# Sixty-seven elementwise operations move from GpSimd to the VectorE in two attention mixers, and the exponential's table is loaded at their start

## The chip, the cores and the metric

One core of a Trainium2 chip runs the whole program. The metric is device time in microseconds (us) of one execution; three executions of the kernel before took 1954.1 to 1957.93 us. [...]

## The reference, cut to what matters

Two transformer layers on 512 tokens of width 1024, all in f32: each layer is half an FFN, a mixer, and half an FFN. The first mixer is "even" (sparse NSA attention beside dilated attention), the second is MLA.

```python
for l in range(2):
    x = x + 0.5 * _swiglu(_rms_norm(x, ffn1_norm[l]), ...)
    h = _rms_norm(x, mix_norm[l])
    x = x + (_even_mixer(h, ...) if l % 2 == 0 else _mla_mixer(h, ...))
    x = x + 0.5 * _swiglu(_rms_norm(x, ffn2_norm[l]), ...)
return _rms_norm(x, final_norm)

def _rope(x, cos, sin):            # rotary positions
    x1, x2 = x[..., :half], x[..., half:]
    return concatenate([x1 * c - x2 * s, x2 * c + x1 * s])

def _probs(scores, mask):          # softmax; every attention uses it
    s = where(mask, scores, -MASK_BIG)
    p = where(mask, exp(s - max(s)), 0)
    return p / sum(p)
```

In the even mixer, 8 NSA heads attend to compressed keys (31 blocks), to selected blocks and to a window; 8 more heads are a mixture of three dilated branches. MLA has 16 heads with low-rank queries and keys.

## The kernel before, in words

Everything is kept transposed: `x` is eight tiles of 128 features x 512 tokens. A matmul in f32 accuracy is three matmuls (`mm3`, lines 150 to 154) on a high part and a low part of both operands. So every operand is split first: ScalarE copies it to the rounded type (`wh`, `qh`, `oh`, ...), and then another engine subtracts that copy from the tile (`wl`, `ql`, `ol`, ...). For weights this is `fetch` (lines 136 and 137).

The stages run in order: FFN, even mixer, FFN, FFN, MLA mixer, FFN, norm. An FFN keeps TensorE on long rows of 128x512 matmuls. A mixer is a software pipeline, `pipe` (line 313): for each head it emits the next head's scores and softmax (`soft`), then the units of work that a plan written by hand (`EVEN`, `MLA`, lines 34 to 46) puts beside this head (projections of queries and keys, values, the compression, output projections), then this head's transposes (`trans`) and its product with the values (`pv`). What is emitted last goes through a scheduler that may move instructions on each engine by its own timing model; each engine then runs its list strictly in order.

Softmax of a head and a block of 128 queries: TensorE writes scores into one of two `pb` banks; the VectorE adds the mask and takes the minimum (line 273, an operation and a read of its accumulator, tile `mn`), which frees the bank; ScalarE takes the exponential (276); the VectorE takes a reciprocal (277); GpSimd scales (281). Other PSUM banks: `pa` (2, projections, queries, output projection), `pt` (3, transposes), `pc` (1, the heads' outputs).

What GpSimd does besides 281, by line:

- `rope` (427): the VectorE multiplies the projection by the cosines (430) and shuffles it (431); GpSimd multiplies the shuffled tile by the sines (432) and adds both (433). 15 calls.
- `finish` (473): a pair of heads is split for the output projection, low part on GpSimd (483). 8 pairs.
- `cmp_probs` (570), twice: softmax on compressed keys. VectorE 583 to 586, exponential on ScalarE (587), product with the mask on GpSimd (588), sum, reciprocal and gate on the VectorE (589 to 592), product with the gate on GpSimd (595), transposes on TensorE (598).
- MLA: one product in the keys' rotary part (650), the low part of a query (708, 16 times) and of a pair of heads (726, 8 times).
- `stack` adds positions for the compression (520, eight operations), `squares` sums squares for the norms (174); both stay.

`out_proj` (381) writes pieces of the output into the two `pa` banks; the VectorE adds each to `x` (397), and the bank is free again. ScalarE loads a table for the exponential before the first exponential of each mixer, at line 276, and one for silu in the FFN after it (238).

Of the kernel before, what the change touches and what calls it, by code (L numbers as in the profile page):

```python
# [3 lines left out]
P = 128  # L4
D, SEQ, FF = 1024, 512, 2816
KT, NF, HF = D // P, FF // P, FF // P // 2
# [17 lines left out]
def raw(ap):  # L24
    return ap.bitcast(F32)
# [46 lines left out]
class Core:  # L72
# [137 lines left out]

    def norm(self, gi):
        xs = [self.split(self.x[k], self.g[:, gi * 8 + k:gi * 8 + k + 1], "x", 8) for k in range(KT)]
        col, row = self.rms(self.x)
        return xs, col, row
# [185 lines left out]
    def even(self, gi):  # L400
        nc, a, kp = self.nc, self.a, self.keep
        with self.tc.tile_pool(name="ev", bufs=1, reuse_waits="tile") as sb:
            xs, rc, R = self.norm(gi)
            CR = sb.tile([P, SEQ], F32, name="CR")
# [22 lines left out]
            def rope(p):  # L427
                t = self.tmp()
                s = self.tmp()
                nc.vector.tensor_tensor(t, p, CR, OP.mult)  # L430
                nc.vector.stream_shuffle(s, p, SHUF8)
                nc.gpsimd.tensor_tensor(s, s, SR, OP.mult)
                nc.gpsimd.tensor_tensor(t, t, s, OP.add)
                return t
# [38 lines left out]
            def finish(pair, j):  # L473

                def f(ps):
                    if j == 0:
                        O[pair] = kp.tile([P, SEQ], F32, name="of")
                    self.fold(sb, ps, O[pair][64 * j:64 * j + 64])
                    if j == 1:
                        h = sb.tile([P, SEQ], F32R, name="oh", bufs=4)  # L480
                        l = sb.tile([P, SEQ], F32R, name="ol", bufs=4)
                        nc.scalar.activation(h, O[pair], AF.Copy)
                        nc.gpsimd.tensor_tensor(l, O[pair], raw(h), OP.subtract)
                        oh[pair] = h, l
                return f
# [84 lines left out]
            def cmp_probs(g):  # L570
# [8 lines left out]
                st = C["st"][g]  # L579
# [8 lines left out]
                nc.gpsimd.tensor_tensor(t, t, mcmp[:, 1].unsqueeze(2).to_broadcast([P, 4, 4, 32]), OP.mult)  # L588
# [6 lines left out]
                nc.gpsimd.tensor_tensor(t, t, sp(st[:, 2]), OP.mult)  # L595
# [22 lines left out]
    def mla(self, gi):  # L618
        nc, a, kp = self.nc, self.a, self.keep
        with self.tc.tile_pool(name="ml", bufs=1, reuse_waits="tile") as sb:  # L620
            xs, rc, R = self.norm(gi)

# [19 lines left out]
            def low(i):  # L642
# [3 lines left out]
                if i == 3:  # L646
# [3 lines left out]
                    nc.gpsimd.tensor_tensor(s, s, cs[:, 1], OP.mult)  # L650
# [46 lines left out]
            def query(h):  # L697
# [10 lines left out]
                nc.gpsimd.tensor_tensor(ql, t, raw(qh), OP.subtract)  # L708
                qs[h] = qh, ql

            def attend(h):
# [5 lines left out]
                def after(ps):  # L717
# [4 lines left out]
                    if j == 1:  # L722
# [3 lines left out]
                        nc.gpsimd.tensor_tensor(l, O[pair], raw(x), OP.subtract)  # L726
# [153 lines left out]
```

## Time and profile before

| | |
|---|---|
| median of three runs | 1957.92 us |
| the runs | 1957.92, 1954.1, 1957.93 us |
| the profiled execution | 1958.47 us |
| its span, first to last instruction | 1956.7 us |
| its mean granted TensorE clock | 0.993 |
| busy in the span: TensorE, VectorE, ScalarE, GpSimd | 1916.9, 1057.6, 754.9, 407.7 us |

The stages lie about here in the span: FFN to 376 us, even mixer to 684, two FFNs to 1398, MLA mixer to 1592, FFN to 1940, final norm to 1957. A row of a window names the stretch and its length, then for each engine the time in which it was busy with its number of instructions, the granted clock, and the share and rate of the DMA engines. A row of a timeline has the start, the time from start to end, the engine, the line and what it writes from what; in brackets the idle time before it. A row of a wait has the total, the number of waits and the longest. Operations on the VectorE that follow each other without a wait start a little before the one ahead has ended, so that rows overlap by some hundredths of a us. Ends of matmuls are modelled.

### The profile page before, as it was taken

How to read it: one execution, taken by the hardware profiler on the slowest of the kernel's cores; microseconds unless marked ns; L12 is line 12 of the kernel's file. 1: busy time of each engine (PE TensorE's matmuls, PEld its weight loads, DVE VectorE, ACT ScalarE, POOL GpSimd, SP SyncE). 2: the span in 40 equal slices, each digit the busy share in tenths (PEclk: the TensorE clock that was granted, in tenths of full speed). 3: DMA queues.
4: the chain of work that ended last, by engine and by line, in shares of the span. 5: the costliest groups of instructions: out<-in, count | busy, mean ns of one | idle time of the engine just before them, and what ended most of it. 6: DMA issues, size and time to landing. Idle time of an engine off the chain costs nothing.

```text
span 1956.7 us, 23295 instructions
## 1 busy us (share of the span) xinstructions
PE 1916.9 (98%) x9086; PEld 1604.4 (82%) x9086; DVE 1057.6 (54%) x1594; ACT 754.9 (39%) x1230; POOL 407.7 (21%) x390
## 2 busy tenths in 40 slices
PE   8999999999999999999999999999999999999997
PEld 6888888878897888888888888888878878888886
DVE  5543444467788754434544543554399765434442
ACT  5321323347586532222333322333388643212231
POOL 4110111164355311001111100111156331101111
PEclk9999999999999999999999999999999999999998
DMA  4333333322111133323232332232310223233331
GB/s 163 97 97 97 97 97 97 117 88 95 47 55 33 44 105 101 97 92 103 94 101 87 97 97 97 97 97 97 122 46 23 65 87 97 97 97 97 97 97 54
DMA packets 49422, 174.37 MB, mean 89 GB/s; under 512 B 5792, under 2 KB 6176, under 8 KB 49312
## 3 DMA queue, kind: packets, MB, share of 16 engines
q1 hardware_dynamic: 47808, 169.64, 27.0%
q0 software_dynamic: 640, 2.10, 0.3%
q8 instruction: 71, 1.16, 0.2%
q10 hardware_dynamic: 864, 1.15, 0.2%
q14 instruction: 39, 0.32, 0.1%
HBM read 170.76 MB, written 2.10 MB: 88 GB/s over the span
## 4 chain that ended last, share of the span: by engine, by line
PE 93%; DVE 4%; ACT 2%; issue 1%; POOL 0%; DMA 0%; DVEq 0%; ACTq 0%; POOLq 0%
PE pa L152 11%; PE pa L153 11%; PE pa L154 11%; PE pb L153 9%; PE pb L154 9%; PE pb L152 9%; PE pt L154 4%; PE pc L154 4%; PE pc L152 4%; PE pt L152 4%; PE pc L153 4%; PE pt L153 4%; PE pc L301 2%; PE pt L290 2%; PE pb L469 1%; DVE wl L137 1%
## 5 line engine op out<-in xcount | busy, mean ns | idle before, releaser
L136 ACT ACTIVATE wh<-w 128x1024 fp32r<-128x1024 f32 (+1 forms) x313 | 331.3, 1059 | 867.0 <-issue 352.1
L137 DVE TENSOR_TENSOR wl<-w,wh 128x1024 fp32r<-128x1024 f32 (+1 forms) x313 | 481.8, 1540 | 235.5 <-ACT wh L136 234.9
L152 PE MATMUL pa<-xh,wh 128*128 128x512 f32 x928 | 364.4, 393 | 8.7 <-ACT xh L161 8.2
L153 PE MATMUL pa<-xl,wh 128*128 128x512 f32 x928 | 363.3, 391 | 0.0
L154 PE MATMUL pa<-xh,wl 128*128 128x512 f32 x928 | 362.9, 391 | 0.0
L240 POOL TENSOR_TENSOR fa<-fs,fu 128x512 f32<-128x512 f32 x88 | 117.5, 1335 | 1043.8 <-DVE fu L236 974.3
L153 PE MATMUL pb<-xl,wh 128*128 128x512 f32 x704 | 275.1, 391 | 0.2
L152 PE MATMUL pb<-xh,wh 128*128 128x512 f32 x704 | 274.8, 390 | 0.0
L154 PE MATMUL pb<-xh,wl 128*128 128x512 f32 x704 | 274.3, 390 | 0.0
L152 PEld LDWEIGHTS pa<-xh,wh 128*128 128x128 f32 x928 | 175.1, 189 | 45.0 <-ACT xh L161 8.2
L236 DVE TENSOR_TENSOR fu<-pb,rrow 128x512 f32<-128x512 f32 x88 | 60.8, 691 | 267.1 <-PE pb L154 267.1
L154 PEld LDWEIGHTS pa<-xh,wl 128*128 128x128 f32 x928 | 175.1, 189 | 36.0
L153 PEld LDWEIGHTS pa<-xl,wh 128*128 128x128 f32 x928 | 175.0, 189 | 36.1 <-DVE xl L162 0.9
L153 PEld LDWEIGHTS pb<-xl,wh 128*128 128x128 f32 x704 | 132.5, 188 | 30.1 <-DVE xl L162 2.6
L152 PEld LDWEIGHTS pb<-xh,wh 128*128 128x128 f32 x704 | 132.4, 188 | 27.8 <-ACT xh L161 0.4
L154 PEld LDWEIGHTS pb<-xh,wl 128*128 128x128 f32 x704 | 132.4, 188 | 27.4 <-DVE wl L137 0.2
L152 PE MATMUL pc<-fah,wh 128*128 128x512 f32 x352 | 136.9, 389 | 0.0
L153 PE MATMUL pc<-fal,wh 128*128 128x512 f32 x352 | 136.9, 389 | 0.0
L154 PE MATMUL pc<-fah,wl 128*128 128x512 f32 x352 | 136.9, 389 | 0.0
L152 PE MATMUL pt<-fah,wh 128*128 128x512 f32 x352 | 136.9, 389 | 0.0
L153 PE MATMUL pt<-fal,wh 128*128 128x512 f32 x352 | 136.9, 389 | 0.0
L154 PE MATMUL pt<-fah,wl 128*128 128x512 f32 x352 | 136.9, 389 | 0.0
(184 smaller groups left out, 2666.0 us busy)
## 6 DMA issues: line engine op xcount, KB each, us to landing
w<-f_g SPq DMA_DIRECT2D x88, 512.0 KB, 3.4
w<-f_u SPq DMA_DIRECT2D x88, 512.0 KB, 3.4
w<-f_d SPq DMA_DIRECT2D x88, 512.0 KB, 3.4
w<-ev_in SPq DMA_DIRECT2D x16, 512.0 KB, 3.4
w<-ev_out SPq DMA_DIRECT2D x8, 512.0 KB, 3.6
w<-mla_out SPq DMA_DIRECT2D x8, 512.0 KB, 3.5
x<-x POOLq DMA_DIRECT2D x8, 256.0 KB, 6.9
w<-ev_vb SPq DMA_DIRECT2D x4, 512.0 KB, 3.5
```

The source lines that it names most:

```text
L136: nc.scalar.activation(h[:, :cols], w[:, :cols], AF.Copy)
L137: nc.vector.tensor_tensor(l[:, :cols], w[:, :cols], raw(h[:, :cols]), OP.subtract)
L152: nc.tensor.matmul(out, wh, xh, start=start, stop=False)
L153: nc.tensor.matmul(out, wh, xl, start=False, stop=False)
L154: nc.tensor.matmul(out, wl, xh, start=False, stop=stop)
L236: nc.vector.tensor_tensor(u, pgu[1], R, OP.mult)
L240: nc.gpsimd.tensor_tensor(a, s, u, OP.mult)
L290: nc.tensor.transpose(ps[:, i * P:(i + 1) * P], pt[:, c:c + P], self.ident)
L301: nc.tensor.matmul(ps[:, q0:], v(kt), PT[j][:, b, :], start=start and kt == 0 and j == 0, stop=stop and kt == 3 and j == 1)
L469: nc.tensor.matmul(ps[:, :n], q[qi][:, qt * P:(qt + 1) * P], kd[ki][j][:, :n], start=j == 0, stop=j == 1)
```

## The change

Sixty-seven operations in eight places get another engine: 432 and 433 (15 each), 483 (8), 588 and 595 (2 each), 650 (1), 708 (16) and 726 (8) are issued on the VectorE. What they compute is the same. A new function `warm_exp` is called in both mixers right after the norm: it takes an exponential of one column into a small tile that nobody reads, so that the exponential's table is loaded there and not at line 276. Line numbers of the changed kernel are 5 higher after `rms`, 6 higher in the even mixer after its norm, and 7 higher in MLA.

```diff
--- before.py
+++ after.py
@@ -207,6 +207,11 @@
     def rms(self, tiles):
         col = self.rstd(self.squares(tiles), D)
         return col, self.spread(col, self.keep.tile([P, SEQ], F32, name="rrow", bufs=2))
+
+    def warm_exp(self):
+
+        e = self.keep.tile([P, 4], F32, name="rcol", bufs=16)
+        self.nc.scalar.activation(e[:, 0:1], self.x[KT - 1][:, 0:1], AF.Exp, scale=0.0)
 
     def norm(self, gi):
         xs = [self.split(self.x[k], self.g[:, gi * 8 + k:gi * 8 + k + 1], "x", 8) for k in range(KT)]
@@ -401,6 +406,7 @@
         nc, a, kp = self.nc, self.a, self.keep
         with self.tc.tile_pool(name="ev", bufs=1, reuse_waits="tile") as sb:
             xs, rc, R = self.norm(gi)
+            self.warm_exp()
             CR = sb.tile([P, SEQ], F32, name="CR")
             SR = sb.tile([P, SEQ], F32, name="SR")
             nc.sync.dma_start(CR, a["cos_p"])
@@ -429,8 +435,8 @@
                 s = self.tmp()
                 nc.vector.tensor_tensor(t, p, CR, OP.mult)
                 nc.vector.stream_shuffle(s, p, SHUF8)
-                nc.gpsimd.tensor_tensor(s, s, SR, OP.mult)
-                nc.gpsimd.tensor_tensor(t, t, s, OP.add)
+                nc.vector.tensor_tensor(s, s, SR, OP.mult)
+                nc.vector.tensor_tensor(t, t, s, OP.add)
                 return t
 
             def halves(j):
@@ -480,7 +486,7 @@
                         h = sb.tile([P, SEQ], F32R, name="oh", bufs=4)
                         l = sb.tile([P, SEQ], F32R, name="ol", bufs=4)
                         nc.scalar.activation(h, O[pair], AF.Copy)
-                        nc.gpsimd.tensor_tensor(l, O[pair], raw(h), OP.subtract)
+                        nc.vector.tensor_tensor(l, O[pair], raw(h), OP.subtract)
                         oh[pair] = h, l
                 return f
 
@@ -585,14 +591,14 @@
                 nc.vector.tensor_reduce(st[:, 0], t, AX.X, OP.min)
                 nc.vector.tensor_tensor(t, t, sp(st[:, 0]), OP.subtract)
                 nc.scalar.activation(t, t, AF.Exp, scale=-1.0)
-                nc.gpsimd.tensor_tensor(t, t, mcmp[:, 1].unsqueeze(2).to_broadcast([P, 4, 4, 32]), OP.mult)
+                nc.vector.tensor_tensor(t, t, mcmp[:, 1].unsqueeze(2).to_broadcast([P, 4, 4, 32]), OP.mult)
                 nc.vector.tensor_reduce(st[:, 1], t, AX.X, OP.add)
                 nc.vector.tensor_scalar(st[:, 1], st[:, 1], 1.0, None, OP.max)
                 nc.vector.reciprocal(st[:, 2], st[:, 1])
                 nc.vector.tensor_tensor(st[:, 2].rearrange("p (a b) -> p a b", b=4),
                                         st[:, 2].rearrange("p (a b) -> p a b", b=4),
                                         C["g"][:, :, 12 * g:12 * g + 12:3], OP.mult)
-                nc.gpsimd.tensor_tensor(t, t, sp(st[:, 2]), OP.mult)
+                nc.vector.tensor_tensor(t, t, sp(st[:, 2]), OP.mult)
                 pt = self.bank("pt")
                 for qt in range(4):
                     nc.tensor.transpose(pt[:, qt * P:(qt + 1) * P], t[:, qt].rearrange("p a b -> p (a b)"),
@@ -619,6 +625,7 @@
         nc, a, kp = self.nc, self.a, self.keep
         with self.tc.tile_pool(name="ml", bufs=1, reuse_waits="tile") as sb:
             xs, rc, R = self.norm(gi)
+            self.warm_exp()
 
 
             CQ = [sb.tile([P, SEQ], F32, name=f"CQ{i}") for i in range(2)]
@@ -647,7 +654,7 @@
                     t, s = c[3] = self.tmp(), self.tmp()
                     nc.vector.tensor_tensor(t, p, R, OP.mult)
                     nc.vector.stream_shuffle(s, t, SHUF16)
-                    nc.gpsimd.tensor_tensor(s, s, cs[:, 1], OP.mult)
+                    nc.vector.tensor_tensor(s, s, cs[:, 1], OP.mult)
                     nc.vector.tensor_tensor(t, t, cs[:, 0], OP.mult)
                     nc.vector.tensor_tensor(t, t, s, OP.add)
                     return
@@ -705,7 +712,7 @@
                 qh = sb.tile([P, SEQ], F32R, name="qh", bufs=3)
                 ql = sb.tile([P, SEQ], F32R, name="ql", bufs=3)
                 nc.scalar.activation(qh, t, AF.Copy)
-                nc.gpsimd.tensor_tensor(ql, t, raw(qh), OP.subtract)
+                nc.vector.tensor_tensor(ql, t, raw(qh), OP.subtract)
                 qs[h] = qh, ql
 
             def attend(h):
@@ -723,7 +730,7 @@
                         x = kp.tile([P, SEQ], F32R, name="xh", bufs=8)
                         l = kp.tile([P, SEQ], F32R, name="xl", bufs=8)
                         nc.scalar.activation(x, O[pair], AF.Copy)
-                        nc.gpsimd.tensor_tensor(l, O[pair], raw(x), OP.subtract)
+                        nc.vector.tensor_tensor(l, O[pair], raw(x), OP.subtract)
                         oh[pair] = x, l
                 return self.job(sb, scores, mcau, PT, lambda: self.bank("pc"),
                                 lambda kt: vs[h // 4][:, kt, h % 4, :], True, True, None, after,
```

The scheduler has put all engines' lists of both mixers in another order. Three places follow.

The VectorE in the even mixer, at the first head's scores. `t` is a rotary tile, `mn` the minima, `mdil` the mask; `kl`, `q` and `wl` are low parts. Before:

```order
L430 TENSOR_TENSOR t<-pa,CR 128x512
L431 STREAM_SHUFFLE t<-pa 128x512
L273 ISA p,mn<-pb,mdil 128x128
L273 ISA mn 128x1
L456 TENSOR_TENSOR kl<-t,kh 64x512
L137 TENSOR_TENSOR wl<-w,wh 128x840
L277 RECIPROCAL mn<-mn 128x1
L446 SCALAR_TENSOR_TENSOR q<-t,q 64x512
L516 TENSOR_TENSOR t<-pa,rrow 128x512
L446 SCALAR_TENSOR_TENSOR q<-t,q 64x512
L273 ISA p,mn<-pb,mdil 128x256
```

The same place in the changed kernel:

```order
L436 TENSOR_TENSOR t<-pa,CR 128x512
L437 STREAM_SHUFFLE t<-pa 128x512
L278 ISA p,mn<-pb,mdil 128x128
L278 ISA mn 128x1
L462 TENSOR_TENSOR kl<-t,kh 64x512
L438 TENSOR_TENSOR t<-t,SR 128x512
L137 TENSOR_TENSOR wl<-w,wh 128x840
L282 RECIPROCAL mn<-mn 128x1
L439 TENSOR_TENSOR t<-t 128x512
L522 TENSOR_TENSOR t<-pa,rrow 128x512
L278 ISA p,mn<-pb,mdil 128x256
```

The rotary product and sum (438, 439) stand in this list now, and the two low parts `q` (446) have moved behind the second minimum.

The VectorE at the first `cmp_probs` of the even mixer, with the output projection's additions to `x`. Before:

```order
L583 TENSOR_TENSOR t<-pt,mcmp 128x512
L585 TENSOR_REDUCE st_2591<-t 128x16
L586 TENSOR_TENSOR t<-t,st_2591 128x512
L446 SCALAR_TENSOR_TENSOR q<-t,q 64x512 x2
L589 TENSOR_REDUCE st_2591<-t 128x16
L590 TENSOR_SCALAR st_2591<-st_2591 128x16
L137 TENSOR_TENSOR wl<-w,wh 128x1024
L591 RECIPROCAL st_2591<-st_2591 128x16
L397 TENSOR_TENSOR x_65<-pa,x_65 128x512
```

In the changed kernel:

```order
L439 TENSOR_TENSOR t<-t 128x512
L489 TENSOR_TENSOR ol<-of,oh 128x512
L282 RECIPROCAL mn<-mn 128x1
L589 TENSOR_TENSOR t<-pt,mcmp 128x512
L282 RECIPROCAL mn<-mn 128x1
L452 SCALAR_TENSOR_TENSOR q<-t,q 64x512
L591 TENSOR_REDUCE st_2593<-t 128x16
L452 SCALAR_TENSOR_TENSOR q<-t,q 64x512
L592 TENSOR_TENSOR t<-t,st_2593 128x512
L137 TENSOR_TENSOR wl<-w,wh 128x1024
L402 TENSOR_TENSOR x_65<-pa,x_65 128x512
L594 TENSOR_TENSOR t<-t,mcmp 128x512
```

The first addition to `x` (397, now 402) stands ahead of the product with the mask (588, now 594) and of the sum that needs it, no longer behind.

The VectorE at the start of the MLA mixer, from the rotary part of the keys (`t`, `cs`) to the first keys. Before:

```order
L652 TENSOR_TENSOR t<-t 128x512
L192 TENSOR_TENSOR rv<-rv,rcol 128x4
L193 TENSOR_SCALAR rv<-rv 128x4
L704 TENSOR_TENSOR t<-pa,CQ_10596 128x512
L677 TENSOR_TENSOR kl_10613<-t,kh_10612 64x512
L677 TENSOR_TENSOR kl_10615<-t,kh_10614 64x512
L196 TENSOR_TENSOR rcol<-rcol 128x4
L704 TENSOR_TENSOR t<-pa,CQ_10597 128x512
```

In the changed kernel:

```order
L659 TENSOR_TENSOR t<-t 128x512
L192 TENSOR_TENSOR rv<-rv,rcol 128x4
L711 TENSOR_TENSOR t<-pa,CQ_10600 128x512
L193 TENSOR_SCALAR rv<-rv 128x4
L684 TENSOR_TENSOR kl_10617<-t,kh_10616 64x512
L711 TENSOR_TENSOR t<-pa,CQ_10601 128x512
L684 TENSOR_TENSOR kl_10619<-t,kh_10618 64x512
L684 TENSOR_TENSOR kl_10613<-t,kh_10612 64x512
L196 TENSOR_TENSOR rcol<-rcol 128x4
L684 TENSOR_TENSOR kl_10615<-t,kh_10614 64x512
L715 TENSOR_TENSOR ql<-t,qh 128x512
L702 TENSOR_TENSOR kl_10613<-pa,kh_10612 64x512
```

The second query's product (704, now 711) stands one low part earlier, and the first query's low part (708, now 715) stands ahead of the first keys' low part (695, now 702).

## Rows read from the trace of the kernel before

**Rows 1.** The profile's page: busy time, share of the span and instructions of each engine.

```profile
PE 1916.9 (98%) x9086; PEld 1604.4 (82%) x9086; DVE 1057.6 (54%) x1594; ACT 754.9 (39%) x1230; POOL 407.7 (21%) x390
```

**Rows 2.** Windows of the two mixers: the even mixer whole, and six stretches.

```profile
384.00:684.00 300.00, 287.31 (x1635) 248.17 (x1635) 235.63 (x579) 188.01 (x417) 145.88 (x154) 0.98 0.19 61
412.00:450.00 38.00, 34.12 (x199) 29.94 (x198) 29.96 (x72) 23.69 (x49) 21.35 (x20) 0.91 0.24 76
490.00:512.00 22.00, 18.94 (x107) 16.27 (x106) 17.44 (x36) 9.55 (x19) 9.14 (x9) 0.92 0.15 48
595.00:620.00 25.00, 20.29 (x119) 16.64 (x119) 22.31 (x56) 14.09 (x34) 12.96 (x14) 1.00 0.13 43
1410.00:1440.00 30.00, 26.23 (x137) 21.68 (x136) 21.66 (x45) 17.60 (x33) 8.69 (x9) 0.94 0.16 53
1440.00:1530.00 90.00, 89.04 (x532) 78.69 (x531) 84.97 (x240) 77.73 (x192) 56.62 (x71) 1.00 0.14 42
1530.00:1592.00 62.00, 61.31 (x307) 50.52 (x306) 44.88 (x80) 31.97 (x60) 20.66 (x19) 1.00 0.19 60
```

**Rows 3.** Waits of TensorE over the span: total us, times, longest.

```profile
PE pa L152 <- DVE x L397: 5.6, 4, 3.1
PE pb L469 <- DVE mn L273: 4.3, 3, 2.9
PE pb L153 <- DVE kl L695: 1.8, 1, 1.8
...
PE pa L364 <- DVE t L704: 1.1, 1, 1.1
```

**Rows 4.** Groups by form: total us, mean ns, then idle time before.

```profile
L432 POOL TENSOR_TENSOR t<-t,SR 128x512 f32<-128x512 f32 x15 | 23.2, 1544 | 38.1 <-DVE t L431 36.6 <-DVE mn L277 1.4
...
L651 DVE TENSOR_TENSOR t<-t,cs 128x512 f32<-128x512 f32 x1 | 1.6, 1562 | 0.0
...
L652 DVE TENSOR_TENSOR t<-t 128x512 f32<-128x512 f32 x1 | 0.7, 676 | 0.0
```

**Rows 5.** Timelines of VectorE and ScalarE at the even mixer's first scores.

```profile
420.82 1.77 DVE L456 TENSOR_TENSOR kl<-t,kh 64x512 fp32r<-64x512 f32 x1
422.62 1.99 DVE L137 TENSOR_TENSOR wl<-w,wh 128x840 fp32r<-128x840 f32 x1
...
425.33 0.68 DVE L446 SCALAR_TENSOR_TENSOR q<-t,q 64x512 fp32r<-64x512 f32 x1 [0.65 <-ACT q L445]
...
427.49 0.42 DVE L273 CUSTOM_DVE_ANT_0 p<-pb,mdil 128x256 f32<-128x256 f32 x1
...
422.20 1.28 ACT L276 ACT_TABLE_LOAD   x1
```

**Rows 6.** Timelines of VectorE and GpSimd at the first compressed softmax.

```profile
499.50 2.85 DVE L446 SCALAR_TENSOR_TENSOR q<-t,q 64x512 fp32r<-64x512 f32 x2
...
503.22 1.23 DVE L137 TENSOR_TENSOR wl<-w,wh 128x1024 fp32r<-128x1024 f32 x1
...
504.52 0.63 DVE L397 TENSOR_TENSOR x<-pa,x 128x512 f32<-128x512 f32 x1
...
500.34 1.46 POOL L588 TENSOR_TENSOR t<-t,mcmp 128x512 f32<-128x512 f32 x1 [0.23 <-ACT t L587]
```

**Rows 7.** ScalarE where the new exponential stands: MLA's timeline, the even mixer's waits.

```profile
1401.75 1.06 ACT L136 ACTIVATE wh<-w 128x1024 fp32r<-128x1024 f32 x1 [5.51 <-issue]
...
ACT v L377 <- PE pa L366: 9.1, 2, 7.9
```

**Rows 8.** Timeline of VectorE at the start of the MLA mixer.

```profile
1428.78 2.37 DVE L677 TENSOR_TENSOR kl<-t,kh 64x512 fp32r<-64x512 f32 x2
```

**Rows 9.** One stretch of the MLA mixer on GpSimd: line 708, then line 726, then line 281.

```profile
1440.00:1530.00 90.00, 19.14 (x14) 1.00 0.14 42
...
1440.00:1530.00 90.00, 6.53 (x6) 1.00 0.14 42
...
L281 POOL TENSOR_SCALAR p<-p,mn 128x512 f32<-128x512 f32 x12 | 10.3, 862 | 7.3 <-DVE mn L277 7.3
```

## The prediction

> **What bounds the kernel now.** I read the page first: TensorE is busy for 1916.9 of 1956.7 us, the VectorE for 54% [rows 1]. So only time in which TensorE waits, or runs at its lower clock, can be won. Next come the windows of the two mixers, the only stages that the change touches. In the even mixer TensorE is idle for 300 - 287.3 = 12.7 us, and 11.7 of them lie in three short stretches: 3.9 at 412 to 450, 3.1 at 490 to 512, 4.7 at 595 to 620 [rows 2]. The MLA mixer has 3.8 at 1410 to 1440 and then 1.0 and 0.7 [rows 2]. Beside the idle time stands the clock. [...] That costs another 38 x 0.09 = 3.4, 22 x 0.08 = 1.8 and 30 x 0.06 = 1.8 us. The four stretches thus lose 7.3, 4.9, 4.7 and 5.6 us, 22.5 in all, about 1.1% of the span: the ceiling, give or take what the modelled ends of matmuls hide.
>
> Then the waits, to see who is late. TensorE waits for the VectorE in all the main ones: for a minimum that frees a score bank (273), for the addition that frees an output bank (397), for a query's product (704) and for a low part of the keys (695) [rows 3]. The VectorE is late for two reasons. GpSimd's operations are long: 1.54 us for a rotary product [rows 4]. And they stretch the VectorE's own: two products of the same shape, both with two tiles in SBUF, took 1.56 us beside GpSimd's line 650 and 0.68 us behind it [rows 4].
>
> **The price of a moved operation.** The trace has no rotary product on the VectorE, but a sum of two 128x512 SBUF tiles in 0.68 us [rows 4]. It is the same kind and size, so I take 0.68 for each; 1.56 [rows 4] is the upper end, where GpSimd works on something else at that time. No reason allows less than 0.68.
>
> **The first scores of the even mixer (7.3 lost).** TensorE waits 2.9 us for the minimum of the second block, which the VectorE begins at 427.49. From 420.82 it did: a low part of keys in 1.77 us, a weight split of 840 columns in 1.99, both stretched, then an idle 0.65 for ScalarE, whose queue held the table load of 1.28 us, and two query low parts and a product of 0.68 each [rows 5]. In the changed list the query low parts stand behind this minimum, and two moved operations before it. Sum in the new order: 0.68 (keys) + 0.68 (product) + 1.23 x 840/1024 = 1.0 (split, at the clean rate of [rows 6]) + 0.1 (reciprocal) + 0.68 (sum) + 0.68 = 3.8 us, in place of 427.49 - 420.82 = 6.7. That is 2.9 earlier, the whole wait. With no long wait left I expect the clock to stay up. Bounds: nothing won, or 7.3. I take -6, since a second, shorter wait remains likely there.
>
> **The two compressed softmaxes (4.9 and 4.7 lost).** At 504.52 the addition that TensorE waits for stands behind two query low parts (2.85 for two, against 1.36 clean), behind the sum that needs GpSimd's 588 (1.46 us), and a split [rows 6]. In the new list it is ahead of 588 and that sum, which takes away 1.5 + about 0.7; but three moved operations come in before it (432, 433, 483), 2.0 us. So the addition gains little, 0.2 us by this sum and more only if the VectorE has spare time ahead. Behind it the softmax no longer crosses to GpSimd and back twice (588, 595). The second one is alike, and its split of 1024 columns no longer meets GpSimd. Bounds: +3.2 (rival below) to -9.6. I take -3.5 for both, nearer the small end, because the sum is.
>
> **The start of the MLA mixer (5.6 lost).** The VectorE loses 1.56 - 0.68 = 0.9 in line 651 [rows 4] and 2.37 - 1.36 = 1.0 in two low parts of the keys' rotary half, beside GpSimd's 708 [rows 8]. Both go. Lines 650 and the first 708 come onto the VectorE ahead of line 695: 2 x 0.68 = 1.4. Net -0.5; the second query's product also stands one operation earlier, -0.7. The waits for 704 and 695 are 2.9 together [rows 3]. Bounds 0 and -5.6; I take -2, 1.2 of these and a part of the clock.
>
> **The middle of the MLA mixer.** Here the change costs. From 1440 to 1530 the VectorE is busy for 84.97 of 90 us, and TensorE for 89.04 [rows 2]: both are full. GpSimd runs 14 of the queries' low parts and 6 of the pairs' there [rows 9]. Moved, they are 20 x 0.68 = 13.6 us on an engine with 5.0 free: 8.6 too much. Behind the stretch the VectorE has 62 - 44.9 = 17.1 us free [rows 2], but a query's low part is needed before its scores; only a pair's can be late, and the plan fixes which projections stand beside which head. Bounds: 0, if the order moves all of the excess behind 1530, and +8.6. I take +4, the middle, as neither is nearer. While it waits in this full queue, a low part holds up the next minima and transposed low parts, and TensorE waits for those.
>
> **Costs of nothing.** The new exponential is a table load of 1.28 us [rows 5] and a short operation, under 1.7 us together. ScalarE is idle for 5.5 us at that place in MLA and for 7.9 us in the even mixer, there waiting for TensorE [rows 7]; without this cover the norm's row would be late by 1.7 in each. The other moved operations of the even mixer are covered: all 42 there (15 + 15 + 8 + 2 + 2) are 28.6 us, and the VectorE has 300 - 235.6 = 64.4 free [rows 2]; if it is not where they need it, +3. The FFNs and the transfers don't change.
>
> **Sum.** -6 - 3.5 - 2 + 4 = -7.5 us. The profiled execution took 1958.47 us, 1.8 beyond its span and 0.5 above the median of the runs. Forecast: **1951.0 us**.
>
> [...] The trace shows an operation held up by another engine's: 1.56 against 0.68 us [rows 4]. [...] Worked out from rows: 281 fills 56.62 - 19.14 - 6.53 = 31.0 of the 90 us, 34%, and a long one takes 0.86 us [rows 2, 9]; 20 x 0.34 x 0.43 = 2.9 us more in MLA, 1953.9 in all. [...]
>
> **The rivals.**
>
> - *The VectorE bounds the MLA mixer: slower.* Place: 1440 to 1530. Price: the full excess of 8.6, and 2.9 for meetings with 281 (20 x 0.34 x 0.43, as above), +11.5; the even mixer wins only its first place, -6, and MLA's start nothing. 1958.5 + 11.5 - 6 = 1964.0. It decides from the point at which the moved low parts, less 5.0 of spare time, find no other work that can be put off. For it: VectorE at 94%. Against it: TensorE is as full, and part of the VectorE's 85 us are waits stretched by GpSimd that go. Chance 0.20.
> - *The wait turns up in the compressed softmax: no change.* On one engine 588, the sum, the gate's operations and 595 now stand in a row with the additions between; the transposes (598) wait for 588 and 595 at 0.68 each and what is between, about 1.6 later each time. -6 + 3.2 - 2 + 4 = -0.8: 1957.7. For it: the short sum above. Against it: the order puts projections ahead of the transposes. Chance 0.22.
> - *All waits close.* -6.5 in the first place, -6 in the softmaxes, -3.5 in MLA's start, nothing lost in its middle: 1942.5. For it: the new order is made with shorter moved operations, and no long GpSimd operation is left but 520. Chance 0.16.
> - My forecast keeps 0.42. That the change doesn't do what it says is excluded: the lists show 67 operations on the other engine and the table load in its new place.
>
> **How the numbers follow.** 0.2% of the median, 3.9 us, is about what a measurement of this kernel can tell from no change. Faster: 0.42 + 0.16 = 0.58; same 0.22; slower 0.20. The range runs from 1938, some us under the third rival for its bounds, to 1964, the first rival; beyond it lie the worse half of that rival and the rest of the ceiling.
>
> **What would show it.** Right: the clock at 412 to 450 is 1.0 and the wait for 273 there is under 1 us; line 651 and the low parts of 677 take 0.7 us; the VectorE is busy for over 95% in MLA's middle and TensorE idle for about 4 us more there. Wrong: in the even mixer TensorE idles as much as before, at 397 or 598, or MLA grows by 8 us or more; or it doesn't grow, and the time falls under 1946.

## The result, and the profile after

The changed kernel is slower: 1969.47 us median of 4 runs (1968.92 to 1969.92) against 1957.86 of the kernel before beside it; ratio 1.0063, 95% interval 1.0051 to 1.0076. That is +12.3 us where -7.5 was forecast. Below, a difference in us is always a ratio less 1, times 1957.5, with the interval of the ratio beside it. The profiled execution took 1969.86 us at the same mean granted clock as that of before, 0.993. Line numbers after the change: 281 is now 286, 273 is 278, 397 is 402; in the even mixer add 6 (432 is 438, 588 is 594), in the MLA mixer 7 (704 is 711, 708 is 715, 726 is 733).

The page's busy row (answers to [rows 1]):

```profile
PE 1924.8 (98%) x9086; PEld 1605.8 (82%) x9086; DVE 1085.7 (55%) x1661; ACT 755.1 (38%) x1232; POOL 317.4 (16%) x323
```

GpSimd lost 90 us of work and the VectorE is busy for only 28 more: the moved operations took 98 us on GpSimd and take 48 there (a query's low part 1405 ns before, 686 now), and its others are stretched less beside GpSimd (old line 651 took 1562 ns beside 650, now 679; the four of 677 took 928 in the mean, now 682). The windows of the mixers (answer to [rows 2]; three stretches between them are new; columns as there):

```profile
384.00:684.00 300.00, 288.98 (x1616) 246.87 (x1615) 252.55 (x621) 185.03 (x416) 89.03 (x112) 0.98 0.19 61
412.00:450.00 38.00, 36.35 (x236) 32.73 (x234) 32.13 (x84) 25.49 (x58) 13.46 (x17) 1.00 0.28 90
450.00:490.00 40.00, 39.64 (x219) 34.33 (x220) 34.92 (x87) 25.91 (x58) 6.53 (x10) 1.00 0.31 98
490.00:512.00 22.00, 19.36 (x114) 16.34 (x114) 20.43 (x45) 9.96 (x22) 3.26 (x5) 1.00 0.19 60
512.00:595.00 83.00, 81.80 (x480) 71.26 (x479) 67.87 (x191) 56.53 (x137) 25.86 (x37) 0.96 0.12 40
595.00:620.00 25.00, 22.42 (x115) 18.37 (x113) 22.19 (x56) 13.02 (x29) 4.84 (x8) 0.93 0.20 64
620.00:684.00 64.00, 61.40 (x324) 50.24 (x325) 54.39 (x134) 42.64 (x102) 26.00 (x31) 1.00 0.11 34
1410.00:1440.00 30.00, 26.85 (x141) 22.69 (x140) 21.33 (x45) 15.85 (x29) 3.94 (x5) 0.94 0.19 54
1440.00:1530.00 90.00, 83.55 (x479) 70.83 (x478) 86.70 (x239) 72.89 (x177) 28.67 (x47) 1.00 0.10 30
1530.00:1592.00 62.00, 61.06 (x312) 50.86 (x311) 50.20 (x103) 36.06 (x73) 12.65 (x17) 1.00 0.22 68
```

Read it against [rows 2] and two more stretches of before:

```profile
450.00:490.00 40.00, 40.00 (x233) 35.41 (x233) 31.77 (x83) 27.29 (x63) 17.91 (x17) 1.00 0.33 106
512.00:595.00 83.00, 83.00 (x511) 74.08 (x509) 67.62 (x194) 60.32 (x144) 37.88 (x49) 1.00 0.17 52
```

The three places that lost time in the even mixer are better: TensorE is 2.2 us busier at 412 to 450 and the clock 1.00 for 0.91; 0.4 and 1.00 for 0.92 at 490 to 512; 2.1 at 595 to 620, though there the clock is now 0.93. But where TensorE had no idle time at all (450 to 490 and 512 to 595) it has some now, and the clock falls to 0.96 at 512 to 595. Over the whole mixer the clock is 0.98 both times: its fall has moved to a later stretch. In MLA's middle TensorE loses 5.5 us, while the VectorE is busy for 96%.

Idle time and clock do not show the whole loss. In the 300 us of the even mixer TensorE is 1.7 us busier at the same clock, yet has 1616 matmuls for 1635; in MLA's middle it has 479 for 532. The ends of matmuls are modelled, so a busy row can hide short waits between them.

Milestones show it better: the additions that end the first and the last head of the even mixer, before and after.

```profile
450.54 0.67 DVE L333 TENSOR_TENSOR of<-pc,t 64x512 f32<-64x512 f32 x1
...
660.47 0.68 DVE L333 TENSOR_TENSOR of<-pc,t 64x512 f32<-64x512 f32 x1 [1.04 <-ACT t L332]
```

```profile
441.74 0.68 DVE L338 TENSOR_TENSOR of<-pc,t 64x512 f32<-64x512 f32 x1 [1.41 <-ACT t L337]
...
663.68 0.68 DVE L338 TENSOR_TENSOR of<-pc,t 64x512 f32<-64x512 f32 x1 [1.46 <-ACT t L337]
```

A lead of 8.8 us has become 3.2 us of delay. Not all of the lead was won time: the stretch from 412 to 450 gained 5.6 us (2.2 of idle time, 38 x 0.09 = 3.4 of clock), the rest is most likely the new order, which ends the first head sooner; by the fourth head the lead is 3.3 (490.98 for 494.31). The same additions for the first and the last head of MLA, before and after:

```profile
1449.99 0.68 DVE L333 TENSOR_TENSOR of<-pc,t 64x512 f32<-64x512 f32 x1
...
1563.16 0.69 DVE L333 TENSOR_TENSOR of<-pc,t 64x512 f32<-64x512 f32 x1 [1.22 <-ACT t L332]
```

```profile
1452.34 0.66 DVE L338 TENSOR_TENSOR of<-pc,t 64x512 f32<-64x512 f32 x1
...
1575.15 0.69 DVE L338 TENSOR_TENSOR of<-pc,t 64x512 f32<-64x512 f32 x1 [1.22 <-ACT t L337]
```

From first to last head MLA takes 122.8 us for 113.2. So of the 11.4 us by which the span grew (1956.7 to 1968.1), 3.2 came with the even mixer and 9.6 between MLA's heads; between and behind these places 1.4 were won. TensorE's waits over the span (answer to [rows 3]):

```profile
PE pa L152 <- DVE x L402: 3.9, 5, 1.9
PE pa L152 <- DVE t L711: 3.2, 3, 1.7
PE pb L475 <- DVE mn L278: 1.9, 3, 0.6
...
PE pb L153 <- DVE kl L702: 1.4, 1, 1.4
...
PE pt L295 <- DVE cl L609: 1.3, 1, 1.3
PE pc L306 <- DVE gt L566: 1.3, 1, 1.3
```

The long waits are shorter, the minimum's 0.6 instead of 2.9, but there are more of them, on new lines. Durations, by form (answer to [rows 4, 8]):

```profile
L438 DVE TENSOR_TENSOR t<-t,SR 128x512 f32<-128x512 f32 x15 | 11.3, 754 | 0.1
L715 DVE TENSOR_TENSOR ql<-t,qh 128x512 fp32r<-128x512 f32 x16 | 10.9, 686 | 0.0
...
L684 DVE TENSOR_TENSOR kl<-t,kh 64x512 fp32r<-64x512 f32 x4 | 2.7, 682 | 0.1
...
L658 DVE TENSOR_TENSOR t<-t,cs 128x512 f32<-128x512 f32 x1 | 0.7, 679 | 0.0
```

The price of 0.68 was right, and the old lines 651 and 677 have shrunk as forecast. What a full VectorE does to TensorE is to be seen in its timeline at 1462, with TensorE's next wait under it:

```profile
1462.01 0.68 DVE L711 TENSOR_TENSOR t<-pa,CQ 128x512 f32<-128x512 f32 x1
1462.61 1.28 DVE L715 TENSOR_TENSOR ql<-t,qh 128x512 fp32r<-128x512 f32 x2
1463.81 0.69 DVE L733 TENSOR_TENSOR xl<-of,xh 128x512 fp32r<-128x512 f32 x1
1464.41 1.22 DVE L137 TENSOR_TENSOR wl<-w,wh 128x1024 fp32r<-128x1024 f32 x1
1465.55 0.69 DVE L715 TENSOR_TENSOR ql<-t,qh 128x512 fp32r<-128x512 f32 x1
...
1466.75 0.68 DVE L711 TENSOR_TENSOR t<-pa,CQ 128x512 f32<-128x512 f32 x1
...
1467.48 0.50 PE L152 MATMUL pa<-cnh,wh 128*128 128x512 f32 x1 [1.69 <-DVE t L711]
```

Line 711 reads the bank that the next projection needs. Between two of them stand three moved low parts of queries and one of a pair, 2.7 us that GpSimd had done beside it.

### The profile page after: what moved, and what is told of

Same layout as the page of the kernel before. It is cut to its first block, busy times and chain, and to the rows that moved or that the text cites. A ratio compares the mean times of both kernels' runs of the same rounds, so it can differ in the third digit from the quotient of the medians.

```text
span 1968.1 us, 23236 instructions
## 1 busy us (share of the span) xinstructions
PE 1924.8 (98%) x9086; PEld 1605.8 (82%) x9086; DVE 1085.7 (55%) x1661; ACT 755.1 (38%) x1232; POOL 317.4 (16%) x323
## 4 chain that ended last, share of the span: by engine, by line
PE 90%; DVE 7%; ACT 1%; issue 1%; DMA 0%; DVEq 0%; POOL 0%; ACTq 0%; POOLq 0%
PE pa L152 11%; PE pa L153 11%; PE pa L154 11%; PE pb L153 8%; PE pb L154 8%; PE pb L152 8%; PE pt L153 4%; PE pc L153 4%; PE pt L154 4%; PE pc L154 4%; PE pt L152 4%; PE pc L152 4%; PE pc L306 2%; PE pt L295 1%; DVE p L278 1%
## 5 line engine op out<-in xcount | busy, mean ns | idle before, releaser
L137 DVE TENSOR_TENSOR wl<-w,wh 128x1024 fp32r<-128x1024 f32 (+1 forms) x313 | 473.6, 1514 | 234.0 <-ACT wh L136 233.5
```

The lines of the kernel that those rows point to most:

```text
L137: nc.vector.tensor_tensor(l[:, :cols], w[:, :cols], raw(h[:, :cols]), OP.subtract)
```

## Experiments

Moves are all of one kind, `nc.gpsimd` to `nc.vector` in one line, so most diffs are short.

**The parts of the change.** First the early exponential alone:

```diff
             xs, rc, R = self.norm(gi)
+            self.warm_exp()
```

> The kernel before, with the early exponential in both mixers and nothing else. Theory (the VectorE's load in the two mixers made the kernel slower; the early table load gained the first scores a little): 1.3 us for the table load that no longer stands in ScalarE's queue ahead of the first scores, so 1956 to 1958. Rival 'table' (the early exponential itself delays the norm's row and so costs): 1.7 us in each mixer, 1960 to 1962.

Measured 1954.92 us, ratio 0.9989 (0.998 to 0.9998), -2.2 us. It gains, more than the theory's 1.3, and the norm's row is not late (383.1 us for 383.2 in the even mixer). Part of the gain goes with the clock: at a mean clock of 0.996 it takes 1953.1 to 1953.4 us and the kernel before 1953.8 to 1954.4, about 0.9 less, but 4 of its 11 executions had that clock and 4 of 27 of before beside them.

Then MLA's part alone:

```diff
-                    nc.gpsimd.tensor_tensor(s, s, cs[:, 1], OP.mult)
+                    nc.vector.tensor_tensor(s, s, cs[:, 1], OP.mult)
...
-                nc.gpsimd.tensor_tensor(ql, t, raw(qh), OP.subtract)
+                nc.vector.tensor_tensor(ql, t, raw(qh), OP.subtract)
...
-                        nc.gpsimd.tensor_tensor(l, O[pair], raw(x), OP.subtract)
+                        nc.vector.tensor_tensor(l, O[pair], raw(x), OP.subtract)
```

> The kernel before, with the MLA mixer's part of the change alone (650, 708, 726 on the VectorE, early exponential there). Theory (load): the MLA mixer's excess as the two traces show it, +7 to +8: 1965 to 1966, with TensorE 5 us more idle in 1440 to 1530 (83.5 busy). Rival 'even' (the even mixer's moves cost all of it and what MLA shows is inherited from it): 1957 to 1959, TensorE 88 or more there. Rival 'sum of both' with an order that happens to suit: anything between, to be read in the window.

Measured 1966.83 us, 1.0051 (1.0039 to 1.0064), +10.0. Its window is that of the whole change, 83.66 against 83.55:

```profile
1440.00:1530.00 90.00, 83.66 (x485) 71.11 (x485) 86.79 (x236) 73.52 (x178) 28.21 (x47) 1.00 0.13 36
```

So MLA's part alone costs most of it, and inherits nothing from the even mixer. The even mixer's part alone (432, 433, 483, 588, 595 and the exponential):

> The kernel before, with the even mixer's part of the change alone (432, 433, 483, 588, 595 on the VectorE, early exponential there). Theory (load): +3 to +4, the even mixer's excess as the two traces show it: 1961 to 1962, the first scores without a wait and 440 to 590 with more. Rival 'even': +11.6, 1969.5. If the forecast of the even mixer (-9.5) held and MLA alone were at fault: 1948.

Measured 1960.41 us, 1.0017 (1.0008 to 1.0026), +3.3. The two add up to 13.3, the whole change is 12.3. The forecast of -9.5 for this mixer fails too. And the whole change with 708 and 726 back on GpSimd:

> The changed kernel, with the 16 queries' low parts and the 8 pairs' low parts of the MLA mixer (708, 726 of the kernel before) back on GpSimd; 650 and both exponentials stay changed. Theory (load in MLA's middle): the MLA mixer is again as it was, so the even mixer's +3 to +4 alone is left, less up to 1.5 at MLA's start: 1960 to 1962. Rival 'order' (the new order of MLA, whichever engine does the low parts, made it slower): 1966 or more. TensorE busy in the 90 us of MLA's middle: 88.5 or more by the theory, under 86 by the rival.

Measured 1961.69 us, 1.0026 (1.0017 to 1.0034), +5.1; TensorE is busy for 89.04 of MLA's 90 us again. So the 24 low parts, with the order that comes with them, are what costs there; which of the two this run does not show, since the lists were made anew.

**Which low parts, and is it the VectorE's time?** 708 alone, then 726 alone:

> The kernel before with the queries' low parts alone (708, 16 of them, 14 in 1440 to 1530) on the VectorE. Theory (load: only what goes beyond the VectorE's spare 5.0 us in MLA's middle costs): 14 x 0.68 = 9.5, less 5.0: +4.5, 1961.5. Rival 'hold-up' (each moved low part waits in the VectorE's queue for ScalarE's copy of the query and holds up the next minimum, so the cost goes by the number of queries and needs no full engine): nearly all of the MLA part's +9.8, 1966.

> The kernel before with the pairs' low parts alone (726, 8 of them, 6 in 1440 to 1530) on the VectorE. Theory (load): 6 x 0.68 = 4.1 us, less than the spare 5.0: no change, 1957, at most +1. Rival 'proportion' (every moved 0.68 us costs what it takes, spare or not): 8 x 0.68 = 5.4 at most, about +3, 1960.

Measured 1967.87 (1.0059, 1.0046 to 1.0072: +11.5) and 1964.49 (1.0037, 1.0025 to 1.005: +7.2). Both miss the theory by far: eight operations of 0.68 us cannot fill an engine with 5.0 us free, yet they cost 7.2. The timelines of the VectorE, of GpSimd and of TensorE in the run with 726 alone show where 2.25 of it go:

```profile
1503.92 1.43 DVE L137 TENSOR_TENSOR wl<-w,wh 128x1024 fp32r<-128x1024 f32 x1
1505.27 1.75 DVE L726 TENSOR_TENSOR xl<-of,xh 128x512 fp32r<-128x512 f32 x1
1506.95 0.68 DVE L704 TENSOR_TENSOR t<-pa,CQ 128x512 f32<-128x512 f32 x1
...
1504.24 2.24 POOL L708 TENSOR_TENSOR ql<-t,qh 128x512 fp32r<-128x512 f32 x1
...
1507.69 0.50 PE L152 MATMUL pa<-xh,wh 128*128 128x512 f32 x1 [2.25 <-DVE t L704]
```

In the new order a weight split and the pair's low part stand ahead of the product that frees the bank, and the low part takes 1.75 us for 0.68 beside GpSimd's 708. Behind the wait the clock falls: 0.94 in 1500 to 1530, another 1.8 us. So two things were mixed here, the VectorE's time and the order, and the next run does not part them either. It is MLA's part with the weights' low parts given to GpSimd in exchange:

```diff
-        nc.vector.tensor_tensor(l[:, :cols], w[:, :cols], raw(h[:, :cols]), OP.subtract)
+        eng = nc.gpsimd if key[0].startswith("mla") else nc.vector
+        eng.tensor_tensor(l[:, :cols], w[:, :cols], raw(h[:, :cols]), OP.subtract)
```

> As the run of MLA's part alone, but the low parts of the weights that the MLA mixer fetches (137) go to GpSimd in exchange: the VectorE loses about as much there (7 x 1.38 = 9.6 us in 1440 to 1530 of before) as it takes up beyond its spare time. Theory (load): +9.8 goes, 1956 to 1959, TensorE busy for 88 us or more in 1440 to 1530. Rival 'hold-up' (where the low parts stand in the VectorE's queue is what costs, not how full it is): still 1964 to 1967, TensorE under 85 there.

Measured 1965.62, 1.0047 (1.0035 to 1.006), +9.2; TensorE 84.68 of 90. That looks like the rival, but the VectorE was not relieved. Its groups by form in MLA (715 and 733 are the low parts):

```profile
L715 DVE TENSOR_TENSOR ql<-t,qh 128x512 fp32r<-128x512 f32 x16 | 16.0, 1001 | 0.0
L733 DVE TENSOR_TENSOR xl<-of,xh 128x512 fp32r<-128x512 f32 x8 | 10.2, 1280 | 0.3 <-ACT xh L732 0.3
```

The worst meeting, in the timelines of the VectorE and GpSimd (138 is the split on GpSimd):

```profile
1461.82 2.85 DVE L715 TENSOR_TENSOR ql<-t,qh 128x512 fp32r<-128x512 f32 x1
...
1461.75 2.38 POOL L138 TENSOR_TENSOR wl<-w,wh 128x1024 fp32r<-128x1024 f32 x1
```

Over the whole mixer the low parts grew by 16 x 0.32 + 8 x 0.58 = 9.8 us. In 1440 to 1530 it was 14 x 0.36 + 5 x 0.42 = 7.1, nearly the 7.5 us of the six splits that the VectorE did there in MLA's part alone. A new order and a GpSimd that is busy for 41.40 of the 90 us, 28.21 in MLA's part alone, spoil such a test.

**The order held.** Therefore the instructions of TensorE, ScalarE and the VectorE were chained in a given order (a dependency without a wait), so that an operation changes its engine and nothing else moves. ORDER lists each engine's instructions of the mixer as they stand in the kernel before, with the moved ones at the place in the VectorE's list where GpSimd had begun them:

```diff
+def hold(tc, nc):
+    ins = {i.name: i for i in nc.cur_bb.bb.instructions}
...
+                    tc.add_manual_dep(ins[name], last, mybir.DependencyInfo(
+                        mybir.DependencyClass.NoSync, mybir.DependencyReason.DATA), reason="order")
...
         Core(tc, ctx, aps).run()
+        hold(tc, nc)
```

All 24 low parts on the VectorE, the order of before:

> The 24 low parts of the MLA mixer (708, 726) run on the VectorE, but from that mixer on every instruction of TensorE, ScalarE and the VectorE keeps its place in the order of the kernel before, and each moved low part stands in the VectorE's queue where GpSimd had begun it. Theory (order: what costs is the new order that the schedule takes when the low parts are VectorE work, not the VectorE's time): within 2 us of before, 1955 to 1959. Rival (load: 20 x 0.68 = 13.6 us on an engine with 5.0 free in 1440 to 1530): +8.6, 1965 to 1967.

Measured 1966.88, 1.0054 (1.0042 to 1.0066), +10.6. The load rival holds, my theory of that moment falls: with every other instruction in its old place the low parts cost about as much as MLA's part did in the new order. The counterpart, the new order with the low parts on GpSimd:

> The counterpart: TensorE, ScalarE and the VectorE keep, from the MLA mixer on, the order of the run with MLA's part alone (+9.8 us), but its 24 low parts are back on GpSimd. Theory (order): still slow, 1963 to 1968. Rival (load): the VectorE has its time back, 1956 to 1959. Between them the test is weaker, since a low part of 1.4 us on GpSimd can be late in an order made for one of 0.68.

Measured 1960.56, 1.0021 (1.0012 to 1.003), +4.1: between the two. The new order costs something when it is not needed, less than the load. Now each group alone with the order of before:

> The 8 pairs' low parts alone (726) on the VectorE, the order of before held as in the run of all 24, each where GpSimd had begun it. Theory (load with a threshold; 6 x 0.68 = 4.1 us is under the spare 5.0 in 1440 to 1530): no change, 1957 to 1958.5, so that the +7.4 of the free schedule is its order. Rival (proportion: each costs its time, 24 cost 9.4, so 8 cost a third): +3.1, 1960.5. Rival (a low part that waits or is stretched costs by itself, whatever the order): +7, 1964.

> The 16 queries' low parts alone (708) on the VectorE, the order of before held. Theory (load with a threshold): 14 x 0.68 - 5.0 = +4.5, 1962. Rival (proportion): 16 of 24 x 9.4 = +6.3, 1963.7. Rival (as with the free schedule): +10.8, 1968.

Measured 1958.94 (1.0005, 0.9997 to 1.0014: +1.0) and 1966.36 (1.004, 1.0028 to 1.0053: +7.8). So of the pairs' 7.2 about 6 were order, and load with a threshold holds for them. For the queries the threshold is too kind: 4.5 expected, 5.5 at the least measured. Proportion fits the queries (6.3) and not the pairs (3.1 expected, 2.7 at the most measured). Last, all 24 with less other work on the VectorE:

```diff
-        nc.vector.tensor_tensor(l[:, :cols], w[:, :cols], raw(h[:, :cols]), OP.subtract)
+        if key[0].startswith("mla"):
+            nc.gpsimd.memset(raw(l[:, :cols]), 0.0)
+        else:
+            nc.vector.tensor_tensor(l[:, :cols], w[:, :cols], raw(h[:, :cols]), OP.subtract)
```

> All 24 low parts on the VectorE with the order of before held (+9.4 us when run so), and the low parts of the weights that the MLA mixer fetches are left out: GpSimd sets them to zero, so that 18 subtractions of 1.2 us, 7 of them in 1440 to 1530 (9.6 us), leave the VectorE. This leaves the low parts of the mixer's weights out of its projections. Theory (load): the 9.4 us go, since 13.6 - 9.6 = 4.0 is under the spare 5.0: 1956 to 1959. Rival (place in the queue: the low part stands between a minimum and what waits for it, however much time the engine has): 1963 or more.

Measured 1961.32, 1.0017 (1.0008 to 1.0026), +3.3. Of 10.6 us 7.3 are gone, so most of the cost goes with how much work stands in the VectorE's queue. 3.3 stay although the sum leaves time spare. MLA's middle in these four runs: all 24, pairs, queries, all 24 without splits.

```profile
1440.00:1530.00 90.00, 84.87 (x485) 72.60 (x484) 86.94 (x237) 72.45 (x177) 27.29 (x46) 0.98 0.12 36
```

```profile
1440.00:1530.00 90.00, 88.60 (x527) 77.64 (x525) 86.73 (x238) 77.29 (x188) 46.35 (x63) 1.00 0.14 42
```

```profile
1440.00:1530.00 90.00, 85.55 (x495) 73.99 (x494) 86.91 (x236) 73.24 (x179) 33.88 (x52) 0.98 0.13 36
```

```profile
1440.00:1530.00 90.00, 86.63 (x514) 75.69 (x514) 84.93 (x245) 76.14 (x185) 34.73 (x56) 1.00 0.14 42
```

In the first three the VectorE stops at about 87 of 90 us: 2 of its 5.0 free us are used, and from there TensorE pays. With 2 in place of 5.0 the sum gives 11.6, 2.1, 7.5 and 2.0 us, each within the interval of its run; but the 2 was read after the runs. In the last run the VectorE has time left at 84.93, and TensorE still idles for 3.4. That speaks for the place in the queue as a second cause, but is not shown: the splits that left had stood in the same queue.

The milestones, one trace each, agree in direction. From MLA's first to its last head it took 113.2 us before and 120.6, 114.4, 118.6 and 115.7 in these four. With the order free it was 122.7 for MLA's part, 119.7 for the pairs and 124.1 for the queries: beside the load the new order costs some 2 to 6 us.

**The pieces of the even mixer.** The rotary lines alone (432 and 433), the compressed softmax alone (588 and 595):

> The kernel before with the rotary products and sums of the even mixer alone (432, 433, 30 operations) on the VectorE, no early exponential. Theory (the even mixer's part gains its first scores by these two lines and gives it back where the 30 operations, 20.4 us, stand between the minima and the additions): 412 to 440 loses 5 us less, 440 to 590 some 5 to 6 more: 1957 to 1959. Rival (the ropes pay and the compressed softmax or the output's low parts, 483, cost): 1951 to 1953.

> The kernel before with the two products of the compressed softmax alone (588, 595; 4 operations) on the VectorE. Forecast's term for these two places: -3.5 (bounds +3.2 and -9.6), 1953.5. Theory (no gain: the additions that TensorE waits for stand behind other VectorE work anyway): within 1.5 us of before, 1956 to 1958.5.

Measured 1955.72 (0.9998, 0.9989 to 1.0007: -0.4), between theory and rival, and 1962.7 (1.0026, 1.0017 to 1.0035: +5.1), outside both. The rotary lines win the first scores as the whole change does (412 to 450: 36.37 busy, clock 1.00) and keep little of it. Four operations that should bring 3.5 cost 5.1. TensorE's waits show one reason (this execution took 1964.71 us, the longest of ten):

```profile
PE pt L598 <- DVE t L595: 3.9, 1, 3.9
```

And the VectorE's timeline at the second softmax:

```profile
602.99 1.16 DVE L588 TENSOR_TENSOR t<-t,mcmp 128x512 f32<-128x512 f32 x1
...
605.38 1.41 DVE L446 SCALAR_TENSOR_TENSOR q<-t,q 64x512 fp32r<-64x512 f32 x2
...
608.25 1.16 DVE L137 TENSOR_TENSOR wl<-w,wh 128x1024 fp32r<-128x1024 f32 x1
...
609.53 0.69 DVE L595 TENSOR_TENSOR t<-t,st 128x512 f32<-128x512 f32 x1
```

595 is now in a row with two query low parts, a split and the additions, and the transposes wait 3.9 us for it; the wait for GpSimd's 595 was 1.3 in the trace of before. Beside these 2.6 us stands the clock, 0.86 at 595 to 620 for 1.00 before: 25 x 0.14 = 3.5. All 42 moved operations with the order of before held, no early exponential:

> The 42 moved operations of the even mixer (432, 433, 483, 588, 595) run on the VectorE, with every other instruction of TensorE, ScalarE and the VectorE in the order of before, and each moved one in the VectorE's queue where GpSimd had begun it; no early exponential. Theory (order): the shorter operations bring what was forecast for this mixer, or a part of it, and nothing is given back: 1949 to 1955. Rival (load: 28.6 us on the VectorE cost where they stand): as the even part alone, 1960 or more.

Measured 1959.68, 1.0008 (0.9998 to 1.0017), +1.6. Not 1949 to 1955, and not clearly slower: in the old order shorter operations bring nothing. At a mean clock of 0.996 (4 of 12 executions) it takes 1954.4 to 1954.7 us, where the kernel before takes 1953.8 to 1954.4: at equal clock the 42 operations cost about 0.4. Its trace adds two things. The minimum of the first scores is still waited for, 2.3 us for 2.9: that this wait goes is the new order's doing more than that of shorter operations. And the second softmax waits hardly longer than before:

```profile
PE pt L598 <- DVE t L595: 1.4, 1, 1.4
```

Here 595 stands ahead of the split, at 603.00. So the 3.9 us above come from where the new order puts 595, not from the engine that does it. Three combinations in search of a faster kernel: table and rotary lines; the even part without 588 and 595; the whole change without these and the 24 low parts:

> The early exponential in both mixers and the rotary lines (432, 433) on the VectorE, everything else as before. If the two gains, -2.1 and -1.4, add: 1953.5. If they are the same gain (both only shorten the wait of the first scores): 1955.

> The even mixer's part of the change (+3.4 us when run alone) without the two products of the compressed softmax (588, 595), which stay on GpSimd. Theory (they are what costs): 1954 to 1956.5, the wait of the transposes (598) for 595 no longer than 1.5 us. Rival (483, or the 30 rotary operations together with it, cost): 1959 or more.

> The whole change without the parts that cost: 588 and 595, and the 24 low parts of the MLA mixer (708, 726 of the kernel before), stay on GpSimd. Theory: the two gains remain, 1953.5 to 1956. Rival (650 or the new order of MLA costs): 1958 or more.

Measured 1955.49 (0.9995, 0.9986 to 1.0003: -1.0), 1958.79 (1.0016, 1.0007 to 1.0025: +3.1) and 1958.33 (1.0014, 1.0005 to 1.0023: +2.7). The first fits one gain, not two that add. The second differs from it in 483 and in MLA's exponential, and is some 4 us slower. In its trace an addition (402) that frees a bank is waited for 1.9 us at 500, for 1.4 in the first, and the clock behind it is 0.84 for 1.00 at 490 to 512: 22 x 0.16 = 3.5 us. So 483, with the order that comes with it, costs as well, mostly by the clock; the third, which has it too, shows the same wait and clock (1.9, 0.84) and misses its theory likewise. The pieces don't add. The lowest median of the study is that of the kernel before with the early exponential alone, 1954.92 us; its interval overlaps with those of the two kernels that have the rotary lines. What of the even mixer's +3.3 is order and what load stays open: +3.3 and +1.6 overlap within their intervals, though the trace with the order held and its executions at 0.996 speak for order.

## Why the prediction was wrong

It fell out of its range and on the wrong side. Two steps failed: the even mixer's other moved operations, taken as covered, and the middle of MLA, where only half of the excess was counted. MLA growing by 8 us or more was one of the prediction's own signs of being wrong; it grew by 9.6 between its heads. Step by step:

- **The price, 0.68 us, and the covers of nothing for the exponential:** right. 754, 686 and 679 ns in the rows above; the exponential alone gains.
- **The first scores, -6:** the mechanism came as described. The longest wait for a minimum is 0.6 us for 2.9, the clock 1.00 for 0.91, and the stretch gained 2.2 + 38 x 0.09 = 5.6 us. But it was a lead, not a gain: it was used up by 663.68.
- **The softmaxes, -3.5:** the two stretches gained 0.4 + 22 x 0.08 = 2.2 and 2.1 - 25 x 0.07 = 0.3 us, most of it. The rival "the wait turns up in the compressed softmax" named the chain (598 behind 588 and 595) on which these operations alone cost 5.1; in the changed kernel, whose order is another, the transposes wait 0.2 us there.
- **The other moved operations of the even mixer, "covered" (28.6 us in 64.4 free; if not, +3):** this step failed. The sum for the mixer was -9.5, measured +3.3, with the terms for the three bad places mostly won. Where the forecast had nothing, at 450 to 490 and 512 to 595, TensorE lost 0.4 and 1.2 us of busy time and 83 x 0.04 = 3.3 us of clock. The 30 rotary operations alone took back most of what they had won (-0.4, at best -2.1), and 483 cost some 4 us in its order. A mean over 300 us says nothing of the moment: a kind of bank has three tiles at most, so TensorE cannot run far ahead, and once the long waits were gone, other operations in the VectorE's queue were late instead (402 for up to 1.9 us, the gate's 566 and 609 for 1.3 each). How much of it is these operations' time and how much the new order stays open.
- **MLA's start, -2:** TensorE is 0.6 busier at the same clock, so most of it did not come.
- **MLA's middle, +4:** this step failed by its size; the mechanism was right. "0, if the order moves all of the excess behind 1530" was no real bound for queries: they are due at once. Measured +10.6 (8.2 to 12.9) with the order held and +10.0 free, so about the whole excess of 8.6 or more, not half of it. Of the spare 5.0 us 2 were used, the new order cost something as well, and "waits stretched by GpSimd that go" were 7 x 0.12 = 0.9 us there (137: 7 at 1376 ns before, 6 at 1254 after).
- **The rival "the VectorE bounds the MLA mixer"** had that place and nearly that price, 11.5, but 2.9 of it were for meetings with line 281, as if the scaling held a low part up for half its own time on average. That was the author's estimate, and no run shows it: 715 takes 686 ns in the mean of 16, and the eight low parts that met the scaling (now 286) in the changed kernel took 0.67 to 0.90 us, 0.3 us above 8 x 0.68 in all. So its price came near by luck. I gave it 0.20, with -6 beside it that did not last.

The same estimate stands in the prediction as 2.9 us on top of the forecast, beside the 1.56 us that line 651 took with 650 at work. What stretched a low part most in these runs was another subtraction: 2.85 us beside GpSimd's split of 2.38 (138), and 1.75 beside GpSimd's 708 of 2.24, for 0.68 alone. Such meetings spoiled the exchange; the changed MLA mixer, whose subtractions are all on the VectorE, has none.

## What to carry to other kernels

A faster engine for an operation is no gain if that engine stands in the way of the one that bounds (here operations of half the time, 48 us for 98, and the kernel 12.3 us slower): add the moved time to the stretch where it falls, count on less than all of the spare time there (here 2 of 5.0 us), and ask which bank-freeing operation now stands behind it in the queue. A stall that goes away early in a pipelined stage is a lead, and counts only if it is still there at the stage's end (here 8.8 us became 3.2 us of delay). Where a scheduler remakes the order, chain the old order before testing a cause: eight moved operations cost 7.2 us with the order free and 1.0 with it held.

## What the hardware showed beside that

In the trace of before TensorE waits 2.92 us for the minimum of the first scores and goes on at 427.98. In windows of 1 us its granted clock is 1.00 up to 426, 0.75 at 426, 0.50 from 427 to 433, 0.84 at 433 and 1.00 from 434. A row of a 128x512 matmul is 0.63 us long while the clock is at 0.50 and 0.39 at 434 (ends are modelled). In the changed kernel this wait is gone; TensorE waits once in 412 to 450, 1.3 us for the gate (566), and the clock of that stretch is 1.00.

The time of one kernel moves by 2 to 5 us with the granted clock. Of 118 executions of the kernel before beside these experiments, 19 had a mean clock of 0.996 and took 1953.8 to 1954.4 us; 95 had 0.993 or 0.994 and took 1956.4 to 1958.8; 4 lay between. Two kernels whose even mixers are the same as before (MLA's part alone, then the 24 low parts with the order held) show it in one stretch: equal busy time, another clock.

```profile
412.00:450.00 38.00, 34.06 (x200) 29.96 (x199) 30.13 (x72) 23.88 (x49) 21.42 (x20) 0.91 0.23 76
```

```profile
412.00:450.00 38.00, 34.06 (x209) 30.18 (x207) 29.87 (x73) 24.57 (x53) 21.56 (x20) 0.96 0.23 77
```

At 0.996 the kernel before, the one with the table alone and the one with the rotary lines alone take 1953.8, 1953.1 and 1953.8 at best. So a good part of the 7 us that the prediction put down to the clock was not the program's to win in each execution, and gains of 1 to 2 us here are partly a matter of how often the clock falls behind the same wait.
